# Encoder block on one core: the first pair's difference formed eight steps sooner, its first product a step sooner, a third key buffer and a later carry copy

## The chip, the cores and the metric

The kernel runs on one core of a Trainium2 chip. The metric is the device time of one execution in microseconds (us); the result of a kernel is the median of its runs. Engines are named as the profile names them: PE multiplies matrices (PEld is its loading of weights), DVE, ACT and POOL work on vectors, SP issues transfers.

## The reference

One layer of an encoder. Each row of `z` is normalised and multiplied by one wide matrix; its columns are queries, keys, values and a gate of a windowed attention, and value, gate and output gate of a depthwise convolution of width 31. Both halves are gated, put side by side and multiplied by an output matrix, and `z` is added.

```python
def hybrid_layer(z, norm_w, w_in, q_norm_w, k_norm_w, sink, conv_w, conv_b, ln_w, ln_b, w_out):
    h = rmsnorm(z, norm_w)
    proj = jnp.einsum('bld,de->ble', h, w_in)
    q, k, v, g_att, c_val, c_glu, g_conv = jnp.split(proj, SPLIT_IDX, axis=-1)
    q = rmsnorm(q.reshape(B, L, N_HEADS, HEAD_DIM), q_norm_w)
    k = rmsnorm(k.reshape(B, L, N_KV_HEADS, HEAD_DIM), k_norm_w)
    v = v.reshape(B, L, N_KV_HEADS, HEAD_DIM)
    att = windowed_gqa(q, k, v, sink).reshape(B, L, W_ATT) * jax.nn.silu(g_att)
    cnv = conformer_conv(c_val, c_glu, conv_w, conv_b, ln_w, ln_b) * jax.nn.silu(g_conv)
    mixed = jnp.concatenate([att, cnv], axis=-1)
    return z + jnp.einsum('ble,ed->bld', mixed, w_out)
```

It runs on two inputs, a prompt of 256 rows and a sample of 2048 rows, each with 16 learned rows in front: 18 blocks of 128 real rows. The model width is 1024, there are 8 query heads and 2 key heads of 64, the attention part and the convolution part are 512 wide each. A query sees the learned keys and the keys at most 128 rows away, with a distance penalty by head, and every softmax row has a learned extra logit.

## The kernel before, in words

**Precision.** A product of float32 matrices is made of three matmuls of rounded parts: a factor is split into a high part (a cast, most often by ACT) and a low part (the factor less the high part, by DVE), and high by high, high by low and low by high are summed (`PASSES`). So each operand that PE takes costs a cast on ACT and a subtraction on DVE first.

**Stages.** The rows are taken in two chunks. In each, the projections run on PE: lines 1024 and 1040, 24 matmuls for a block or half block. Beside them DVE makes the convolution, 31 instructions for each of four channel groups (line 1107, one tap each, `y`); they are handed out by credit, some after each projection. The last 113 columns of a group of the first chunk are kept for the second by a copy on ACT into `ycarry` (line 1118).

After a key block's projection, ACT squares and sums (`sqk`), POOL makes the inverse root (`rqk`, lines 179 and 180), DVE forms the normalised keys `kn` (line 1198), PE transposes them (`kt`, line 1208), ACT makes the high part `ks` (line 1210) and DVE the low part (line 1211), and two transfers store them to `kd`. A query block goes the same way up to `qs` (line 1171), which is stored to `qd`.

From 584.9 us (the first `S`) the attention runs, in stages of eight slots: `slot_step` does in each slot the actions of a table (`acts`), one bank of transposes and its products (`bank`, `pv`, line 623, of the block before), the products with the output matrix (`product`, line 729) from the table `JOBS`, and the scores of the block ahead (`scores`). For each head group `kv` of a block: the scores `S` leave PSUM through DVE (line 531, `sb`), ACT makes exponentials (line 543), POOL multiplies by the inverse sums (`pm` line 560, `sb` line 569, four instructions), PE transposes (`pT_c`, `pT_m`, `pT_x`), ACT and DVE split those into `ptiles` (lines 605, 606 and 595 to 597, the last one POOL's), and PE multiplies them with the values (`O`, line 623, with `vc`, `vm` and so on). `merge` then adds the halves (`at`, line 645 on DVE) and multiplies by the gate (line 651 on POOL).

**Output products.** Blocks 2p and 2p+1 are a pair p. Some of the products are made from sums and differences, so that one product serves two blocks: `c1` of one block's convolution part, `s3` of the difference of the two convolution parts, `s2` and `s4` of further differences with the attention parts, `t0`, `t1` and `s1` likewise. `mix_diff` (line 706, POOL) forms the difference into `temp(0)`; `two_parts` (lines 687 and 688) splits an operand on ACT and DVE; the product of `c1` leaves PSUM into `kept(0)` (in the trace `keptFalse`), that of `s2` into `kept(1)`. `merge` of the pair's first block subtracts the difference from its attention part (line 654) and adds the attention part to the convolution part (line 656). The first pair has earlier steps in the table than the others, since no pair is in front of it.

**Order.** A scheduler decides the order of the instructions on the engines from their order in the program and a table of costs, at first on every engine, from the opening of the attention on all but POOL (`MAN1`), later on all but POOL and PE (`MAN2`), which then follow the program. `later(k, f)` puts `f` off by k ticks of the program, `with_rest(f)` holds `f` back until a tile called `rest` exists. `merge` puts itself off by a tick as long as the pair's difference hasn't been issued. Within one engine instructions run in their order, so a waiting one holds all behind it.

Of the kernel before, what the change touches and what calls it, by code (L numbers as in the profile page):

```python
# [12 lines left out]
F32R = mybir.dt.float32r  # L13
BF16 = mybir.dt.bfloat16
AF = mybir.ActivationFunctionType
ALU = mybir.AluOpType
AX = mybir.AxisListType

P = 128
# [111 lines left out]
def hymba_kernel(  # L131
# [61 lines left out]
    def later(k, f):  # L193
        due.setdefault(clock[0] + k, []).append(f)
# [438 lines left out]
    def merge(b, kv):  # L633
        p, r = divmod(b, 2)
        if "rest" not in cst or (kv == 1 and b not in att) or p not in diff:
            return later(1, lambda: merge(b, kv))
        o = opj[b, kv]
        if kv == 0:
            att[b] = pool["b"].tile([P, 4, P], F32, tag="at", name=f"at{b}")
        at = att[b]  # L640
        pr = slice(2 * kv, 2 * kv + 2)
        tmp = pool["b"].tile([64, 4, P], F32, tag="tmp", name=f"tmp{b}_{kv}", bufs=1)
        nc.scalar.copy(tmp, o[64:128])
        for par in range(2):
            nc.vector.tensor_tensor(  # L645
                at[64 * par : 64 * par + 64, pr, :].rearrange("p a (i q) -> p a i q", q=QB),
                o[0:64].rearrange("p i (a c q) -> p c a i q", a=2, c=2)[:, par],
                tmp.rearrange("p i (a c q) -> p c a i q", a=2, c=2)[:, par],
                op=ALU.add,
            )  # L650
        nc.gpsimd.tensor_tensor(at[:, pr, :], at[:, pr, :], gat[b][:, pr, :], op=ALU.mult)  # L651
        part = at[:, pr, :]
        if kv == 0 and r == 0:
            nc.gpsimd.tensor_tensor(temp(1), part, temp(0), op=ALU.subtract)
            total = cnt[b][:, 0:NS, :]
            nc.gpsimd.tensor_tensor(total, total, part, op=ALU.add)
            work = [("t0", part), ("s2", temp(1)), ("s1", total)]
        elif kv == 0:
            nc.gpsimd.tensor_tensor(temp(1), part, temp(1), op=ALU.subtract)
            work = [("t1", part), ("s4", temp(1))]  # L660
        else:
            work = [(("t", r), part)]

        for name, x in work:
            later(2 + (name == "s4"), lambda name=name, x=x: two_parts(name, x))
# [4 lines left out]
    def temp(i):  # L670
        if not temps:
            temps.extend(gp.tile([P, NS, P], F32, tag="sq4", name=f"temp{k}", bufs=2) for k in range(2))
        return temps[i]
# [16 lines left out]
    def with_rest(f):  # L690
        pending.append(f)
        while "rest" in cst and pending:
            pending.pop(0)()
# [8 lines left out]
    def mix_conv(b):  # L702
        nc.gpsimd.tensor_tensor(cnt[b], cnt[b], gct[b], op=ALU.mult)

    def mix_diff(p):
        nc.gpsimd.tensor_tensor(temp(0), cnt[2 * p + 1][:, 0:NS, :], cnt[2 * p][:, 0:NS, :], op=ALU.subtract)
        diff[p] = True

    banks = []
# [51 lines left out]
    for p in range(NB // 2):  # L761
        b0, b1 = 2 * p, 2 * p + 1
        for rel, f in (
            (5 - (p == 0), lambda b1=b1: load_mix(b1)),
            (6 - 2 * (p == 0), lambda b0=b0: load_mix(b0)),
            (9 + 3 * (p == 0), lambda p=p: load_x(p, (0, 1))),
            (11 - 7 * (p == 0), lambda b1=b1: mix_conv(b1)),
            (12 - 8 * (p == 0), lambda b0=b0: mix_conv(b0)),
            (13, lambda p=p: with_rest(lambda: mix_diff(p))),
            (12 + 2 * (p == 0), lambda p=p: load_x(p, (1, 1))),  # L770
            (13 - 4 * (p == 0), lambda b1=b1: two_parts("c1", cnt[b1][:, 0:NS, :])),
            (14, lambda: with_rest(lambda: two_parts("s3", temp(0)))),
            (17, lambda b0=b0: two_parts(("c", 0), cnt[b0][:, NS:4, :])),
            (17, lambda p=p: load_x(p, (0, 0))),
            (20, lambda b1=b1: two_parts(("c", 1), cnt[b1][:, NS:4, :])),
            (18, lambda p=p: load_x(p, (1, 0))),
            (18, lambda p=p: add_kept(p, (1, 1), 0)),
            (20, lambda p=p: add_kept(p, (0, 0), 1)),
            (21, lambda p=p: add_kept(p, (1, 0), 0)),
        ):  # L780
            acts.setdefault(16 * p + rel, []).append(f)
        for rel, name, es in JOBS:
            to = late_jobs if name == "s3" else jobs
            rel -= p == 0 and name == "c1"
            if p == LAST and name in ("t1", (1, 0)):
                for c0 in (0, 256):
                    to.setdefault(16 * p + rel, []).append((p, name, es, c0, 256))
            else:
                to.setdefault(16 * p + rel, []).append((p, name, es))

    def slot_step(s_, slot):
        a, bb = s_, s_ - 1
        has_a, has_b = a < NB, 0 <= bb < NB
        steps = PLAN if has_b else []
        if slot == 0:
            if a + 1 < NB:
                load_q(a + 1)
                load_k(a + 1)
        if slot == 1 and has_b and s_ > 1:
            load_ga(bb)  # L800
        if slot == VSLOT and 0 < a < NB:
            load_v(a)
        t = 8 * s_ + slot
        with_rest(lambda: None)
        for f in acts.get(t, ()):
            f()
        if slot < len(steps) and steps[slot]:
            bank(bb, *steps[slot])
        for job in jobs.get(t, ()):
            product(*job)  # L810
        if has_a:
            scores(a, slot // 4, slot % 4)
        if slot == (3 if s_ == 1 else QSLOT) and a + 1 < NB:
            q_prep(a + 1)
        for job in late_jobs.get(t, ()):
            product(*job)
        tick(2400)
# [44 lines left out]
    if True:  # L862
# [222 lines left out]
        def conv(c, j, part):  # L1085
            yo = 0 if c == 0 else YC
            o0, o1 = (0, YN)
            n = o1 - o0

            def alloc():  # L1090
                yt[c, j] = yp.tile([P, YW], F32, tag="y", name=f"y{c}_{j}")
                if c == 1:
                    nc.scalar.copy(yt[c, j][:, 0:YC], ycarry[:, j, :])

            def tap(k):
                y, u = yt[c, j], us[c, j]
                if k == 0:
                    nc.vector.tensor_scalar(
                        y[:, yo + o0 : yo + o1],
                        u[:, o0:o1],  # L1100
                        cw[:, j, 0:1],
                        cb[:, j : j + 1],
                        op0=ALU.mult,
                        op1=ALU.add,
                    )
                else:
                    nc.vector.scalar_tensor_tensor(  # L1107
                        y[:, yo + o0 : yo + o1],
                        u[:, o0 + k : o1 + k],
                        cw[:, j, k : k + 1],  # L1110
                        y[:, yo + o0 : yo + o1],
                        op0=ALU.mult,
                        op1=ALU.add,
                    )
                if k == TAPS - 1:
                    left[c, part] -= 1
                    if c == 0:
                        nc.scalar.copy(ycarry[:, j, :], y[:, YN - YC : YN])

            conv_q[j % 2].append((0, alloc))  # L1120
            if c == 0:
                nc.gpsimd.tensor_copy(carry[:, j, :], us[0, j][:, UWID - 30 : UWID])
            left.setdefault((c, part), NJ)
            for k in range(TAPS):
                conv_q[j % 2].append((1.04 * n + 135, lambda k=k: tap(k)))
# [58 lines left out]
        def kv_block(ws, g, o, rows, b):  # L1184
# [21 lines left out]
            def fin2():  # L1206
                pt = psum.tile([P, 512], F32, tag="d", name=f"kt{b}")
                nc.tensor.transpose(pt[:, :rows], kn[:rows].rearrange("p a e -> p (a e)"), ident[:rows, :rows])
                ks = sp.tile([P, 2 * P], F32R, tag="ks", name=f"ks{b}")
                nc.scalar.mul(ks[:, :rows], pt[:, :rows], kscale[:, 0:1])  # L1210
                nc.vector.scalar_tensor_tensor(
                    ks[:, rows : 2 * rows], pt[:, :rows], kscale[:, 0:1], ks[:, :rows], op0=ALU.mult, op1=ALU.subtract
                )
                to = (kmd if b < 0 else kd[b]).rearrange("(h p) k l n -> p h k (l n)", h=2)
                for kv in range(KV):
                    part = ks[HD * kv : HD * kv + HD, : 2 * rows].bitcast(F32)
                    store(to[:, :, kv, :], part.unsqueeze(1).to_broadcast([HD, 2, 2 * rows]))
# [264 lines left out]
```

## Time and profile before

| what | us |
|---|---|
| the runs | 945.50, 946.75, 1397.23 |
| their median | 946.75 |
| the profiled execution, as a whole | 944.26 |
| its span, first to last instruction | 942.5 |
| PE busy | 929.3 |
| DVE busy | 782.4 |
| ACT busy | 448.5 |
| POOL busy | 370.0 |

A row of the timeline has the start in us, the length of the row in us, the engine, the line, the operation, the tiles written and read with their shape, how many instructions the row holds, and in brackets the idle time of the engine just ahead of it with what ended that. Instructions of an engine overlap a little, so the spacing from start to start is shorter than the lengths. The granted clock of PE is 1.000 in this execution.

### The profile page before, as it was taken

To read this page: it belongs to the slowest core of one execution; us is meant where nothing else is said; L and a number is where in the kernel's file an instruction comes from. 1 tells how busy PE (TensorE), PEld (TensorE's weight loads), DVE (VectorE), ACT (ScalarE), POOL (GpSimd) and SP (SyncE) were. 2 spreads that over 40 slices of the span, in tenths; PEclk is the share of its full clock that TensorE was granted. 3 is DMA by queue.
4 is the path that set the end of the run, shared out by engine and by line. 5 is a ranking of instruction groups with operands and counts; after the bars stand their busy time and mean duration, and the time that the engine had idled before them with its cause. 6 is when DMAs were issued, how large, how long until landed. Compare 5 with 4: busy or idle time off the path is not lost.

```text
span 942.5 us, 16872 instructions
## 1 busy us (share of the span) xinstructions
PE 929.3 (99%) x5734; PEld 878.1 (93%) x5734; DVE 782.4 (83%) x1340; ACT 448.5 (48%) x1231; POOL 370.0 (39%) x553
## 2 busy tenths in 40 slices
PE   9999999999999999999999999999999999999998
PEld 8999999999899999999999999977888888888887
DVE  5479999998989889999996554689788888897884
ACT  7442221353456770011111355667677676776772
POOL 3320100184668610000000354687665465556644
PEclk9999999999999999999999999999999999999999
DMA  8579775686565562223333688996556665665421
GB/s 297 178 245 361 249 256 179 207 301 229 126 198 172 186 257 90 90 96 111 117 115 115 198 280 271 381 373 186 171 172 190 176 198 152 183 197 169 144 87 55
DMA packets 146342, 182.80 MB, mean 194 GB/s; under 512 B 40944, under 2 KB 106816, under 8 KB 146128
## 3 DMA queue, kind: packets, MB, share of 16 engines
q1 hardware_dynamic: 146256, 181.72, 58.9%
q8 instruction: 45, 0.74, 0.3%
q14 instruction: 41, 0.34, 0.1%
HBM read 115.83 MB, written 65.85 MB: 193 GB/s over the span
## 4 chain that ended last, share of the span: by engine, by line
PE 85%; DVE 5%; DMA 4%; POOL 3%; issue 1%; SPq 1%; ACT 1%; DVEq 0%; POOLq 0%; ACTq 0%
PE pj L1024 41%; PE yb L729 18%; PE pj L1040 10%; PE O L623 5%; PE S L473 4%; DMA cd<-zn 2%; PE pT_m L589 2%; PE pT_c L589 1%; PE pT_x L589 1%; PE warmup L1257 1%; DVE xt L933 1%; DVE y L1107 1%; POOL sb L569 1%; PE qT L473 1%; DMA wraw<-in_w_in 1%
## 5 line engine op out<-in xcount | busy, mean ns | idle before, releaser
L1024 PE MATMUL pj<-xh,ws 128*128 128x384 f32 (+1 forms) x1536 | 396.7, 339 | 0.1
L1107 DVE SCALAR_TENSOR_TENSOR y<-us,cw,y 128x1167 f32<-128x1167 f32 x240 | 329.6, 1425 | 0.5
L1024 PEld LDWEIGHTS pj<-xh,ws 128*128 128x128 f32 x1536 | 280.1, 188 | 0.5 <-ACT xh L1272 0.4
L1024 PE MATMUL pj<-xl,ws 128*128 128x384 f32 (+1 forms) x768 | 260.9, 340 | 0.1
L1040 PE MATMUL pj<-ws,xh 128*128 128x256 f32 (+1 forms) x880 | 164.7, 284 | 4.3 <-DVE qs L1171 2.5
L1024 PEld LDWEIGHTS pj<-xl,ws 128*128 128x128 f32 x768 | 144.1, 188 | 0.5 <-DVE xl L962 0.4
L1040 PEld LDWEIGHTS pj<-ws,xh 128*128 128x128 f32 (+1 forms) x880 | 136.4, 187 | 5.5 <-issue 2.7
L729 PE MATMUL yb<-wo,rest 128*128 128x512 f32 (+1 forms) x498 | 132.1, 399 | 0.0
L1040 PE MATMUL pj<-ws,xl 128*128 128x256 f32 (+1 forms) x440 | 124.2, 282 | 0.0
L729 PEld LDWEIGHTS yb<-wo,rest 128*128 128x128 f32 x498 | 86.9, 189 | 15.3
L1132 ACT ACTIVATE go<-pj 128x384 f32<-128x384 f32 x48 | 23.5, 490 | 151.5 <-PE pj L1024 137.9
L543 ACT ACTIVATE sb<-sb,nm 128x304 f32<-128x304 f32 (+5 forms) x144 | 77.8, 540 | 26.9 <-DVE nm L531 25.1
L179 POOL TENSOR_SCALAR ssk<-ssk 128x2 f32<-128x2 f32 x18 | 10.3, 574 | 204.3 <-ACT sqk L1146 204.1
L569 POOL TENSOR_SCALAR sb<-sb,es 128x304 f32<-128x304 f32 (+5 forms) x144 | 73.0, 524 | 38.4 <-PE pT_x L589 20.6
L1040 PEld LDWEIGHTS pj<-ws,xl 128*128 128x128 f32 (+1 forms) x440 | 82.2, 187 | 0.3
L531 DVE CUSTOM_DVE_ANT_0 sb<-S,bias,vec 128x304 f32<-128x304 f32 (+5 forms) x144 | 73.7, 515 | 9.3 <-PE S L473 8.1
L179 POOL TENSOR_SCALAR ssq<-ssq 128x4 f32<-128x4 f32 (+2 forms) x55 | 30.4, 552 | 92.5 <-ACT xn L887 70.8
L473 PE MATMUL S<-kw,q 128*128 128x304 f32 (+5 forms) x288 | 63.1, 303 | 0.7 <-issue 0.5
L473 PEld LDWEIGHTS S<-kw,q 128*128 128x128 f32 x288 | 52.1, 188 | 11.5 <-ACT keptFalse L747 0.7
L729 PE MATMUL yb<-wo,ptiles 128*128 128x512 f32 x216 | 60.2, 407 | 1.9 <-ACT ptiles L687 1.4
L651 POOL TENSOR_TENSOR at<-at,ga 128x256 f32<-128x256 f32 x36 | 26.6, 740 | 76.0 <-DVE at L645 76.0
L740 DVE TENSOR_TENSOR yo<-yb,yo 128x512 f32<-128x512 f32 (+1 forms) x55 | 37.1, 674 | 15.4 <-PE yb L729 15.2
(162 smaller groups left out, 1456.1 us busy)
## 6 DMA issues: line engine op xcount, KB each, us to landing
wd<-ws SPq DMA_DIRECT2D x36, 512.0 KB, 5.8
ws<-wd SPq DMA_DIRECT2D x36, 512.0 KB, 5.7
wraw<-in_w_in SPq DMA_DIRECT2D x52, 256.0 KB, 6.1
xn<-in_z SPq DMA_DIRECT2D x18, 512.0 KB, 5.4
gd<-go SPq DMA_DIRECT2D x48, 192.0 KB, 2.1
yo<-in_z SPq DMA_DIRECT2D x36, 256.0 KB, 3.4
wo<-wod SPq DMA_DIRECT2D x18, 512.0 KB, 7.8
out_y<-yo SPq DMA_DIRECT2D x35, 256.0 KB, 2.5
```

The lines of the kernel that those rows point to most:

```text
L179: nc.gpsimd.tensor_scalar(src, src, scale, eps, op0=ALU.mult, op1=ALU.add)
L473: r = f(*a, **k)
L531: nc.vector.tensor_tensor_reduce(out=sb[:, n, c0:c1], in0=ps[:, 0:w], in1=cst["bias"][:, kv, at + c0 : at + c1], scale=1.0, scalar=nsnk[:, ...
L543: nc.scalar.activation(sb[:, n, c0:c1], sb[:, n, c0:c1], AF.Exp, bias=nm[:, n : n + 1], scale=-1.0, accum_out=rs[:, n : n + 1],)
L569: nc.gpsimd.tensor_scalar(sb[:, k, a0:a1], sb[:, k, a0:a1], es[:, k : k + 1], 1.0, op0=ALU.mult, op1=ALU.mult)
L589: nc.tensor.transpose(pt[: c1 - c0, n, :], sbt[b, kv][:, n, c0:c1], ident)
L623: nc.tensor.matmul(opj[b, kv][:, n0:n1], t[:r, kv, :], p[:r, n0:n1], start=(k == "c" and i == 0), stop=(k == "x" and i == len(work) - 1),)
L729: nc.tensor.matmul(ps[:, :n], x[mi][:, i, :], w[wi], start=((name, e) in OPENS and k == 0), stop=(done and e == es[-1] and k == 2), skip_g ...
L740: nc.vector.tensor_tensor(y, ps[:, :n], y, op=ALU.add)
L1024: nc.tensor.matmul(ps[:, :n], ws[:, d, wi, P * half_i : P * half_i + P], x[xi][:, d, o : o + n], start=(k == 0), stop=(k == 3 * ND - 1),)
L1040: nc.tensor.matmul(ps[:rows, :UW], x[xi][:, d, o : o + rows], ws[:, d, wi, :], start=(k == 0), stop=(k == 3 * ND - 1),)
L1107: nc.vector.scalar_tensor_tensor(y[:, yo + o0 : yo + o1], u[:, o0 + k : o1 + k], cw[:, j, k : k + 1], y[:, yo + o0 : yo + o1], op0=ALU.mul ...
```

## The change

Five edits.

1. The first pair's difference is issued at step 5 and no longer at step 13, without being held back for `rest`, and it is written into `kept(1)` instead of `temp(0)` (`diff_c`). Line 654 reads it there.
2. The split of the operand of `s3` is issued at step 10 instead of 14 for the first pair, for no pair held back.
3. The first pair's product `c1` is taken two steps sooner than the other pairs', and no longer one.
4. The query preparation of the stage `s_ == 3` is done in slot 5 instead of 6.
5. The copy into `ycarry` is put off by eight ticks and then keeps its program order; the tile `ks` has three buffers and no longer two.

```diff
@@ merge
-            nc.gpsimd.tensor_tensor(temp(1), part, temp(0), op=ALU.subtract)
+            nc.gpsimd.tensor_tensor(temp(1), part, diff_c(p), op=ALU.subtract)
@@
+    def diff_c(p):
+        if p:
+            return temp(0)
+        return kept(1)[:, : NS * P].rearrange("p (j n) -> p j n", n=P)
+
     def mix_diff(p):
-        nc.gpsimd.tensor_tensor(temp(0), cnt[2 * p + 1][:, 0:NS, :], cnt[2 * p][:, 0:NS, :], op=ALU.subtract)
+        nc.gpsimd.tensor_tensor(diff_c(p), cnt[2 * p + 1][:, 0:NS, :], cnt[2 * p][:, 0:NS, :], op=ALU.subtract)
         diff[p] = True
@@ the table of actions
-            (13, lambda p=p: with_rest(lambda: mix_diff(p))),
+            (13 - 8 * (p == 0), lambda p=p: mix_diff(p) if p == 0 else with_rest(lambda: mix_diff(p))),
...
-            (14, lambda: with_rest(lambda: two_parts("s3", temp(0)))),
+            (14 - 4 * (p == 0), lambda p=p: two_parts("s3", diff_c(p))),
@@ the table of products
-            rel -= p == 0 and name == "c1"
+            rel -= 2 * (p == 0 and name == "c1")
@@ slot_step
-        if slot == (3 if s_ == 1 else QSLOT) and a + 1 < NB:
+        if slot == (3 if s_ == 1 else 5 if s_ == 3 else QSLOT) and a + 1 < NB:
@@ conv
-                        nc.scalar.copy(ycarry[:, j, :], y[:, YN - YC : YN])
+                        carry_y = lambda: nc.scalar.copy(ycarry[:, j, :], y[:, YN - YC : YN])
+                        later(8, lambda: tc.keep_in_program_order(carry_y()))
@@ kv_block
-                ks = sp.tile([P, 2 * P], F32R, tag="ks", name=f"ks{b}")
+                ks = sp.tile([P, 2 * P], F32R, tag="ks", name=f"ks{b}", bufs=3)
```

The new lines shift the line numbers of the changed kernel by 5 (from line 706 of before), and by 6 or 7 further down.

How the instructions stand, in three places. First POOL, where the first pair's first `merge` comes. Here `sb_5908` holds the scores of block 1 with its weights `es_0`, `at` is the merged attention part of block 0, `cn_6237` and `cn_6241` are the convolution parts of blocks 1 and 0. Before:

```order
L560 TENSOR_TENSOR pm_0_6684<-sb_5908,es_0_6456 128x128
L569 TENSOR_SCALAR sb_5908<-sb_5908,es_0_6456 128x272
L569 TENSOR_SCALAR sb_5908<-sb_5908,es_0_6456 128x240
L569 TENSOR_SCALAR sb_5908<-sb_5908,es_0_6456 128x208
L569 TENSOR_SCALAR sb_5908<-sb_5908,es_0_6456 128x176
L530 MEMSET sb_5900 128x32
L706 TENSOR_TENSOR temp_6718<-cn_6237,cn_6241 128x256
L651 TENSOR_TENSOR at_6737<-at_6737,ga_6343 128x256
L654 TENSOR_TENSOR temp_6719<-at_6737,temp_6718 128x256
L656 TENSOR_TENSOR cn_6241<-cn_6241,at_6737 128x256
L597 TENSOR_TENSOR ptiles<-ptiles,vec 128x512
```

And in the changed kernel:

```order
L651 TENSOR_TENSOR at_6738<-at_6738,ga_6345 128x256
L560 TENSOR_TENSOR pm_0_6688<-sb_5908,es_0_6458 128x128
L654 TENSOR_TENSOR temp_6745<-at_6738,kept_6299 128x256
L656 TENSOR_TENSOR cn_6241<-cn_6241,at_6738 128x256
L569 TENSOR_SCALAR sb_5908<-sb_5908,es_0_6458 128x272
L569 TENSOR_SCALAR sb_5908<-sb_5908,es_0_6458 128x240
L569 TENSOR_SCALAR sb_5908<-sb_5908,es_0_6458 128x208
L569 TENSOR_SCALAR sb_5908<-sb_5908,es_0_6458 128x176
L530 MEMSET sb_5900 128x32
L597 TENSOR_TENSOR ptiles<-ptiles,vec 128x512
```

The difference is gone from this row; it stands 25 instructions sooner, behind the inverse root `rqq_9`. `merge` no longer waits for it, so its gate (L651), its difference (L654) and its sum (L656) now stand ahead of the four multiplications of `sb_5908`, which were ahead of them.

Second PE at the same place. `yb_6726` before and `yb_6702` now is the bank of the product `c1` (operands `wa`) and of `s3` (operand `wo_6364`, now `wo_6366`); `O_1` is the output of block 0's second head group. Before:

```order
L623 MATMUL O_0_6509<-ptiles,vm 128x512
L589 MATMUL pT_m_6693<-ident,sb_5904 128x128 x4
L623 MATMUL O_1_6701<-ptiles,vc_5912 128x512 x2
L585 MATMUL pT_x_6724<-ident,pm_1_6462 128x128
L729 MATMUL yb_6726<-wa_6297,ptiles 128x512 x3
L729 MATMUL yb_6726<-wa_6341,ptiles 128x512 x3
L473 MATMUL S_1_2_6734<-kw_5892,q_1_6353 128x208 x2
L473 MATMUL S_1_3_6752<-kw_5892,q_1_6353 128x176 x2
L623 MATMUL O_1_6701<-ptiles,vm_5913 128x512 x2
L589 MATMUL pT_c_6767<-ident,sb_5908 128x128 x4
L473 MATMUL S_0_0_6775<-kw_5891,q_2_6621 128x176 x2
L729 MATMUL yb_6726<-wo_6364,ptiles 128x512 x6
```

And in the changed kernel:

```order
L623 MATMUL O_0_6511<-ptiles,vm 128x512
L734 MATMUL yb_6702<-wa_6297,ptiles 128x512 x3
L734 MATMUL yb_6702<-wa_6343,ptiles 128x512 x3
L589 MATMUL pT_m_6697<-ident,sb_5904 128x128 x4
L623 MATMUL O_1_6713<-ptiles,vc_5912 128x512 x2
L585 MATMUL pT_x_6733<-ident,pm_1_6464 128x128
L473 MATMUL S_1_2_6735<-kw_5892,q_1_6355 128x208 x2
L473 MATMUL S_1_3_6753<-kw_5892,q_1_6355 128x176 x2
L623 MATMUL O_1_6713<-ptiles,vm_5913 128x512 x2
L589 MATMUL pT_c_6768<-ident,sb_5908 128x128 x4
L473 MATMUL S_0_0_6776<-kw_5891,q_2_6625 128x176 x2
L734 MATMUL yb_6702<-wo_6366,ptiles 128x512 x6
```

The six matmuls of `c1` went ahead of the transposes `pT_m` and the two products with `vc`; `pT_c` of block 1 (which reads the multiplied `sb_5908`) still stands ahead of `s3`.

Third ACT, 15 us sooner in the program, where `qr_14` is a query block just projected and `pT_c` and `pT_m` belong to block 0. Before:

```order
L552 ACTIVATE es_1_6247<-nm_1_6245,vec 128x4
L1165 COPY qr_14_6502<-pj_6477 128x256
L1141 ACTIVATE sqq_14_6505<-pj_6477 128x256
L605 CAST ptiles<-pT_c_6449 128x512
L605 CAST ptiles<-pT_m_6515 128x512
```

And in the changed kernel:

```order
L552 ACTIVATE es_1_6247<-nm_1_6245,vec 128x4
L687 CAST ptiles<-kept_6299 128x256
L1171 COPY qr_14_6504<-pj_6479 128x256
L1147 ACTIVATE sqq_14_6507<-pj_6479 128x256
L605 CAST ptiles<-pT_c_6451 128x512
L605 CAST ptiles<-pT_m_6517 128x512
```

The cast of the high part of `s3` now stands here, ahead of the query copy and of the two casts that PE's products with `vc` and `vm` need; before it stood behind them all.

## The prediction

> **What bounds the kernel now.** I began with the page: how much of the span is PE busy?
>
> ```profile
> span 942.5 us, 16872 instructions
> PE 929.3 (99%) x5734; PEld 878.1 (93%) x5734; DVE 782.4 (83%) x1340; ACT 448.5 (48%) x1231; POOL 370.0 (39%) x553
> ```
>
> PE is the bound, with 99% of the span. The change takes no matmul away and adds none, so it can only touch PE's idle time, which is 942.5 - 929.3 = 13.2 us in all. A measurement of this kernel tells about 2% from no change, here 18.9 us. Even with every idle moment gone the time would not leave that band, so the question is how many of the 13 us go. The waits of PE, largest first (total, times, longest):
>
> ```profile
> PE pj L1040 <- DVE qs L1171: 2.5, 2, 2.1
> PE pj L1040 <- ACT ycarry L1118: 1.5, 1, 1.5
> PE yb L729 <- ACT ptiles L687: 1.4, 1, 1.4
> ```
>
> These look like the aims of the edits: the carry copy, the operand of `s3`, and a query block that is behind a key block's ring of buffers. For each I looked in the timeline for what really ends last there. The rows shown from here on are picked from the timeline. Where a row of PE begins late, the loss in the stream is a little more than the idle time it shows, because the row before it no longer overlaps; I take idle time plus 0.2 as the loss.
>
> **The carry copy (edit 5, first half).** Around 245 us:
>
> ```profile
> 241.27 4.11 DVE L1107 SCALAR_TENSOR_TENSOR y<-us,cw,y 128x1167 f32<-128x1167 f32 x3
> ...
> 245.30 0.28 DVE L1198 TENSOR_TENSOR kn<-pj,rqk 128x128 f32<-128x128 f32 x1
> 245.41 0.29 ACT L1118 COPY ycarry<-y 128x113 f32<-128x113 f32 x1 [0.30 <-DVE y L1107]
> ...
> 245.72 0.36 PE L1040 MATMUL pj<-ws,xh 128*128 128x256 f32 x1 [1.53 <-ACT ycarry L1118]
> ```
>
> The copy does end last, at 245.70, but PE takes a PSUM bank of a key block here, and what frees it is `kn`, which ends at 245.58 behind three taps of DVE (4.11 us) that run without a gap. Nothing PE needs comes from `ycarry`. Putting the copy off takes 0.29 us from ACT in front of the squares of the next blocks, and those have time; DVE has the same order of taps and `kn` here as before. Value 0; upper end 0.1 (245.70 - 245.58), lower end 0. Its other copy in the table is followed, ten us on, by the longest wait:
>
> ```profile
> 289.37 4.89 POOL L962 TENSOR_TENSOR xl<-xt,xh 128x384 fp32r<-128x384 f32 x4
> ...
> 295.09 1.99 POOL L180 TENSOR_TENSOR rqq<-ssq,half 128x4 f32<-128x4 f32 x2
> ...
> 298.57 0.36 PE L1040 MATMUL pj<-ws,xh 128*128 128x256 f32 x1 [2.11 <-DVE qs L1171]
> ```
>
> That `qs` needs `rqq`, and POOL makes it only after four splits of the next rows' input (4.89 us). Neither is touched, so these 2.1 + 0.2 us stay. Value 0; upper end 0.3, the length of the copy (0.29) that ACT may hold the squares up by.
>
> **The third buffer of `ks` (edit 5, second half).** With two buffers ACT waits until the store of the block two before has landed:
>
> ```profile
> 265.55 1.98 POOL L180 TENSOR_TENSOR rqq<-ssq,half 128x4 f32<-128x4 f32 x2
> ...
> 266.19 0.37 ACT L1210 ACTIVATE ks<-kt,kscale 128x128 fp32r<-128x128 f32 x1 [3.61 <-DMA kd<-ks]
> ...
> 266.59 0.35 DVE L1211 SCALAR_TENSOR_TENSOR ks<-kt,kscale,ks 128x128 fp32r<-128x128 f32 x1 [1.18 <-ACT ks L1210]
> ...
> 266.85 0.41 DVE L1171 TENSOR_TENSOR qs<-pj,rqq 128x256 f32<-128x256 f32 x1
> ...
> 267.42 0.36 PE L1040 MATMUL pj<-ws,xh 128*128 128x256 f32 x1 [0.43 <-DVE qs L1171]
> ```
>
> This is the one place where that wait reaches PE: ACT stood 3.61 us, DVE's low half 1.18 us behind it, `qs` behind that, and PE 0.43 us behind `qs`. The third buffer takes ACT's wait away. Then `qs` waits for the next cause, its `rqq`, the first of the two in the POOL row, done at about 265.55 + 0.99 = 266.54. So `qs` starts at 266.55 instead of 266.85: **0.3 us** gained. Bounds: 0 (POOL's end is rough) and 0.6 (0.43 + 0.2, all of it).
>
> **The difference and `s3` (edits 1 to 3).** Before, PE stands three times at the first pair:
>
> ```profile
> 612.61 0.84 DVE L645 TENSOR_TENSOR at<-O,tmp 64x256 f32<-64x256 f32 x2
> ...
> 612.75 0.51 PE L623 MATMUL O<-ptiles,vc 128*128 128x512 f32 x1 [0.56 <-DVE ptiles L606]
> ...
> 613.50 0.40 POOL L560 TENSOR_TENSOR pm<-sb,es 128x128 f32<-128x128 f32 x1 [3.38 <-DVE at L645]
> ...
> 614.00 1.73 POOL L569 TENSOR_SCALAR sb<-sb,es 128x272 f32<-128x272 f32 x4
> ...
> 615.52 0.60 PE L589 MATMUL pT_c<-ident,sb 128*128 128x128 f32 x4
> ...
> 615.76 0.73 POOL L706 TENSOR_TENSOR temp<-cn,cn 128x256 f32<-128x256 f32 x1
> ...
> 616.45 0.73 POOL L651 TENSOR_TENSOR at<-at,ga 128x256 f32<-128x256 f32 x1
> ...
> 617.32 0.39 ACT L687 CAST ptiles<-temp 128x256 fp32r<-128x256 f32 x1
> ...
> 617.76 0.74 PE L729 MATMUL yb<-wo,ptiles 128*128 128x512 f32 x2 [1.44 <-ACT ptiles L687]
> ...
> 617.93 0.73 POOL L656 TENSOR_TENSOR cn<-cn,at 128x256 f32<-128x256 f32 x1
> ...
> 618.12 0.82 DVE L688 TENSOR_TENSOR ptiles<-temp,ptiles 128x256 fp32r<-128x256 f32 x1
> ...
> 618.63 1.22 POOL L597 TENSOR_TENSOR ptiles<-ptiles,vec 128x512 fp32r<-128x512 f32 x1
> ...
> 619.00 1.20 PE L729 MATMUL yb<-wo,ptiles 128*128 128x512 f32 x4 [0.51 <-DVE ptiles L688]
> ...
> 620.04 0.39 PE L623 MATMUL O<-ptiles,vm 128*128 128x512 f32 x1
> ```
>
> The losses are 0.56 at `O` (low half of `pT_c` late), 1.44 at `s3`'s first matmuls (its high half) and 0.51 at the others (its low half); with 0.2 each, about 3.1 us. All three causes go: `c1` now stands ahead of the late `O` (six matmuls at a spacing of 0.74 - 0.51 = 0.23, 1.4 us in all, more than 0.76), and `s3`'s parts are ready ten us early. So far the change would gain 3.1 us.
>
> But look at the POOL rows. From 613.50, just behind DVE's `at` (ends 613.45), POOL runs without a gap to 618.63 + 1.22 = 619.85, and the last of it, L597, is what `O` with `vm` at 620.04 needs: the stream of PE is tied to POOL's queue at that end. The change takes one thing out of it, the difference (spacing 615.76 to 616.45, 0.69), and moves the merge's three instructions ahead of the four multiplications of `sb`. So by the same durations: gate 613.5 to 614.2, `pm` to 614.7, L654 (like L651 and L656) to 615.4, L656 to 616.1, four multiplications to 617.85, memset, L597 to 619.1. And `pT_c` of block 1 needs those multiplications. It ran at 615.52 before; PE will be there at 615.52 - 0.76 = 614.8 and finish it at about 617.9, so it stands about 2.2 us less what the first three transposes fill. Behind it in PE's queue are one score and the six matmuls of `s3`: 617.9 + 0.3 + 6 x 0.23 = 619.6. Then `O` with `vm` starts at 619.6 where it was 620.04.
>
> So the wait at `s3` turns into a wait at `pT_c`, and the gain is **0.5 us**. Bounds: 3.1, if the multiplications are no later than before; and below nothing -1.0, next paragraph.
>
> **What the early difference adds.** ACT's cast of it stands right ahead of what PE needs for block 0:
>
> ```profile
> 598.94 1.02 POOL L180 TENSOR_TENSOR rqq<-ssq,half 128x4 f32<-128x4 f32 x1
> 598.99 0.37 ACT L1165 COPY qr<-pj 128x256 f32<-128x256 f32 x1 [0.83 <-PE pj L1040]
> ...
> 599.53 0.59 ACT L605 CAST ptiles<-pT_c 128x512 fp32r<-128x512 f32 x1
> ...
> 602.44 0.39 PE L623 MATMUL O<-ptiles,vc 128*128 128x512 f32 x1
> ```
>
> POOL comes to the difference behind this `rqq` and a memset, at about 600.1, and needs 0.7: done at 600.8. ACT, which was free, now waits for it; its cast takes a spacing of 0.4, the copy and the square 0.54 (598.99 to 599.53), and the cast of `pT_c` ends at 600.8 + 0.4 + 0.54 + 0.59 = 602.3, 2.2 us later than before. `O` with `vc` at 602.44 needs it; it now stands two projection matmuls further down, some 0.2 us. The cover is 0.14 + 0.2, about 0.35 us. I take 0; if it is gone, each further us is PE's. A second inverse root in front of the difference (1.3 us, from the row of 1.02 with its 0.19 and gaps) would cost 1.0.
>
> One sign that POOL's and DVE's rows lengthen each other is in the rows already shown: the low half at 618.12 took 0.82 beside POOL's sum, an equal one later, with no sum of POOL beside it, took half:
>
> ```profile
> 620.05 0.41 DVE L688 TENSOR_TENSOR rest<-temp,rest 128x256 fp32r<-128x256 f32 x1
> ```
>
> [...]
>
> **The query preparation (edit 4).**
>
> ```profile
> 654.24 0.51 PE L473 MATMUL S<-kw,q 128*128 128x304 f32 x2 [0.54 <-issue]
> ...
> 655.31 1.23 POOL L597 TENSOR_TENSOR ptiles<-ptiles,vec 128x512 fp32r<-128x512 f32 x1
> ...
> 656.59 0.51 PE L623 MATMUL O<-ptiles,vm 128*128 128x512 f32 x1 [0.44 <-POOL ptiles L597]
> ```
>
> The wait at 654.24 is for the split of block 4's queries and goes with an earlier slot, 0.54 + 0.2. But two us on PE waits for POOL's L597, at the end of a run of POOL that has hardly a gap (span, busy time and instructions of POOL in that stretch):
>
> ```profile
> 641.85:656.54 14.69, 14.34 (x21) 1.00 0.62 182
> ```
>
> Nothing of that run is moved, so PE comes there 0.7 sooner and waits 0.7 longer. Value 0, ends 0 and 0.8.
>
> **The sum.** 0 + 0.3 + 0.5 + 0 + 0 = 0.8 us gained. The profiled execution took 944.26 us (1.8 more than its span) and would take 943.5. The two runs near it are 945.5 and 946.75, so the three executions lie 2.5 us apart and their middle is 945.5: 945.5 - 0.8 = **944.7 us**.
>
> **Rivals.**
>
> *A, the waits really vanish* (15%). If the multiplications of `sb` aren't on the path (DVE's `at` earlier, or POOL's spans shorter than they look) the three waits at the first pair are worth 3.1, the third buffer 0.6, the queries 0.7: 4.4 us, and 941.1. For it: POOL's idle 3.38 us ahead of 613.50, which the gate could use if DVE's `at` came sooner. Against it: `at` has its own row at 612.61, behind `O` and two DVE rows that aren't moved. With the waits at 245.72 and 298.57 gone as well (1.7 and 2.3) it would be 8.4 us, 937.1; DVE's taps and POOL's splits speak against that.
>
> *B, slower* (20%). ACT's wait for the early difference, in front of the casts of `pT_c` and `pT_m`. It decides as soon as the difference lands 0.35 us later than I have it. If one more inverse root goes first, PE loses 1.0, and if a DVE row is stretched as the low half above was (0.82 against 0.41) 0.4 more; less the gain at the other places, 0.8, that is 0.6 us slower, 946.1; with the `pT_c` wait a full us worse than reckoned, 947.1. For it: behind the waiting cast stand the query copy, which frees a projection bank, and the casts, and PE's `O` waits for these. Against it: ACT stood 0.83 us ahead of the copy at 598.99 anyway.
>
> *C, no gain at all* (10%). The spans of POOL are what they are, `qs` waits for an `rqq` that ends later than its row's middle, and the first pair's chain loses its 0.5 to one more memset. 945.5.
>
> The forecast as worked out, within half a us of 944.7, has 55%.
>
> **Range and chances.** The bounds of the terms: best 0.1 + 0.3 + 0.6 + 3.1 + 0.8 = 4.9 gained (940.6), worst 0.5 - 1.0 - 1.0 = 1.5 lost without the gains elsewhere (947.0). The middle of three runs moves by up to 1.25 either way without any change (945.5 to 946.75). I give 940.5 to 947.5; A's far end of 937 stays out. Slower or faster by over 2% (926.6 or 964.4 from 945.5, or the same from the median 946.75) isn't reached by any case: 97% within 2%, 2% faster, 1% slower, for what the trace doesn't show.
>
> **What would show it.** In the changed kernel's profile PE busy should stay at 929 and its idle time go from 13.2 to about 12.4. Right, step by step: no wait of PE on ACT's `ptiles` of line 687 and none at `O` near 612; in its place a wait of about 2 us of PE at `pT_c` (L589) released by POOL's `sb` (L569); the `qs` wait at 267 shorter by 0.3; the wait at 245.7 still there, now put down to `kn`; the one at 298.6 still 2.1; the one at 654 gone and that at 656.6 up to 1.1. Wrong, if PE has no wait at `pT_c` near 616 (then A), or if a wait appears at 602 to 604 at `O`, released by ACT or DVE `ptiles` (then B).

## The result: 948.2 us, slower by half a per cent

| | before | changed |
|---|---|---|
| median, us | 944.03 (19 runs) | 948.22 (19 runs) |
| ratio, 95% interval | | 1.0046, 1.0038 to 1.0055 |
| profiled execution: span, us | 942.5 | 945.4 |
| its mean granted clock | 1.000 | 0.996 |

The 4.2 us are well inside the 2% band and well outside the uncertainty of these runs. Forecast was a gain of 0.8 us, with a range up to 947.5. One execution of the changed kernel (1850 us) and two of before (1397 and 1132 us) were far off; they stand in these medians and are left out of the ratio.

The page of the changed kernel differs from that of before in a row that the prediction doesn't use, the granted clock of PE in 40 slices:

```profile
span 945.4 us, 16870 instructions
PE 930.4 (98%) x5734; PEld 877.3 (93%) x5734; DVE 782.4 (83%) x1340; ACT 448.0 (47%) x1231; POOL 373.6 (40%) x553
PEclk9999999999999999999999999989999999999999
```

One slice has an 8, and PE, with the same matmuls, is busy 1.1 us longer. PE's waits (total, times, longest):

```profile
PE pj L1045 <- DVE qs L1177: 1.9, 1, 1.9
PE pT_c L589 <- POOL sb L569: 1.6, 1, 1.6
PE pj L1045 <- ACT ycarry L1123: 1.5, 1, 1.5
PE lnu L273 <- DVE zn L267: 1.5, 2, 1.0
...
PE pj L1045 <- ACT sqq L1152: 0.4, 1, 0.4
PE yb L734 <- DVE rest L688: 0.4, 1, 0.4
PE S L473 <- issue: 0.4, 1, 0.4
```

The waits of `s3` on ACT and DVE are gone and the wait at `pT_c` is there, as forecast. Three are new that I had not forecast: `lnu` for `zn`, `yb` for a low half of line 688, and `pj` for ACT's `sqq` at the place of the third buffer. And here is the first pair, PE and then POOL:

```profile
614.77 0.50 PE L623 MATMUL O<-ptiles,vm 128*128 128x512 f32 x1 [0.34 <-DVE ptiles L606]
616.88 1.88 PE L589 MATMUL pT_c<-ident,sb 128*128 128x128 f32 x4 [1.61 <-POOL sb L569]
618.41 0.71 PE L473 MATMUL S<-kw,q 128*128 128x176 f32 x2
618.92 2.83 PE L734 MATMUL yb<-wo,ptiles 128*128 128x512 f32 x6
621.54 0.63 PE L623 MATMUL O<-ptiles,vm 128*128 128x512 f32 x1
```

```profile
613.47 0.73 POOL L651 TENSOR_TENSOR at<-at,ga 128x256 f32<-128x256 f32 x1 [3.78 <-PE pT_x L585]
614.16 0.40 POOL L560 TENSOR_TENSOR pm<-sb,es 128x128 f32<-128x128 f32 x1
614.52 0.73 POOL L654 TENSOR_TENSOR temp<-at,kept 128x256 f32<-128x256 f32 x1
615.21 0.73 POOL L656 TENSOR_TENSOR cn<-cn,at 128x256 f32<-128x256 f32 x1
615.91 2.32 POOL L569 TENSOR_SCALAR sb<-sb,es 128x272 f32<-128x272 f32 x4
```

POOL's queue runs as worked out (gate at 613.47, multiplications from 615.91, where 613.5 and 616.1 had been put), but its four multiplications take 2.32 us instead of 1.73. And the six matmuls of `s3` take 2.83 us where six of `c1` took 1.65 before. The granted clock of the two stretches, after span, busy time and instructions of PE, says why:

```profile
613.01:616.42 3.41, 1.82 (x9) 1.00 1.03 412
616.42:623.25 6.83, 6.27 (x18) 0.50 1.04 410
```

After a stretch in which PE waits twice, the clock is halved for 6.83 us. Half of what PE did from 618.4 (when `pT_c` was through) to 623.25 is lost: 4.8 / 2 = 2.4 us.

To see where the rest goes, the same transposes are compared in the two traces (start in the changed kernel less start in before, us):

```
start in before      234   293   303   526   578   604   623   640   660   927
offset             -1.11 -1.13 -1.32 -0.45 +0.11 -0.14 +2.33 +2.26 +2.78 +2.88
```

The first 1.1 us are in the load at the start, which no edit touches. Lost are 0.9 between 303 and 526, 0.6 between 526 and 578, 2.5 between 604 and 623 and 0.5 between 640 and 660; gained 0.2 at 298 and 0.25 before 604. One execution of each is a small base, so the experiments were timed in five rounds, with the kernel before on the same chip.

### The profile page after: what moved, and what is told of

Its sections match the earlier page's. It is cut to its first block, busy times and chain, and to the rows that moved or that the text cites. A ratio compares the mean times of both kernels' runs of the same rounds, so it can differ in the third digit from the quotient of the medians.

```text
span 945.4 us, 16870 instructions
## 1 busy us (share of the span) xinstructions
PE 930.4 (98%) x5734; PEld 877.3 (93%) x5734; DVE 782.4 (83%) x1340; ACT 448.0 (47%) x1231; POOL 373.6 (40%) x553
## 5 line engine op out<-in xcount | busy, mean ns | idle before, releaser
L179 POOL TENSOR_SCALAR ssq<-ssq 128x4 f32<-128x4 f32 (+2 forms) x55 | 34.1, 620 | 93.0 <-ACT xn L892 71.0
L651 POOL TENSOR_TENSOR at<-at,ga 128x256 f32<-128x256 f32 x36 | 26.5, 737 | 79.4 <-DVE at L645 75.7
```

Of the source, the lines that this page charges most:

```text
L179: nc.gpsimd.tensor_scalar(src, src, scale, eps, op0=ALU.mult, op1=ALU.add)
```

## The experiments

**Two halves of the change.** Edits 1 to 3 alone, which are the first four pieces of the diff above (`diff_c`, the two rows of the table, `c1`'s step):

```diff
-            (13, lambda p=p: with_rest(lambda: mix_diff(p))),
+            (13 - 8 * (p == 0), lambda p=p: mix_diff(p) if p == 0 else with_rest(lambda: mix_diff(p))),
...
-            rel -= p == 0 and name == "c1"
+            rel -= 2 * (p == 0 and name == "c1")
```

> Edits 1 to 3 alone (early difference, early operand of s3, c1 a step sooner). Clock theory: in the changed kernel PE's waits at the first pair are joined into one stretch of about 3 us with little work (1.6 us idle at pT_c), after which the granted clock is 0.5 for 6.8 us, which costs half of that, 3.4 us; the waits themselves get about 1 us shorter. So this kernel should be 2.3 to 2.8 us slower than before, with a mean clock of 0.996 to 0.998 and a slice at half clock near 617 us. Rival (the half clock is an accident of the profiled execution, the waits decide): 0.5 us faster than before, clock 1.000.

Measured: 945.84, ratio 1.0019 (1.0008 to 1.0030), 1.8 us slower; the granted clock was 0.998 or less in 12 executions of 12. The clock theory has the sign and the clock right and the size somewhat high; the rival is out.

Edits 4 and 5 alone:

```diff
-        if slot == (3 if s_ == 1 else QSLOT) and a + 1 < NB:
+        if slot == (3 if s_ == 1 else 5 if s_ == 3 else QSLOT) and a + 1 < NB:
...
+                        later(8, lambda: tc.keep_in_program_order(carry_y()))
...
+                ks = sp.tile([P, 2 * P], F32R, tag="ks", name=f"ks{b}", bufs=3)
```

> Edits 4 and 5 alone (query slot, carry copy, third key buffer). Order theory: the extra time outside the first pair comes from these: PE's lnu transposes and the stages around them are put in another order between 293 and 345 us, where a new wait of 1.0 us for zn stands, another of 0.45 at 570 us, and 0.5 at 660 us, less 0.2 at 267 and 297: 1.5 to 1.9 us slower than before, clock 1.000. Rival (these are chance of one execution, only the named waits move): 0.3 us faster than before.

Measured: 945.61, ratio 1.0025 (1.0011 to 1.0039), slower by 1.5 us by the medians and 2.4 by the ratio. The order theory has the sign; its size is reached only with some help of the clock (executions at 1.000 are 1.2 us above before's at 1.000). One piece of it is not from these edits: the wait for `zn` near 570 us is in 12 of the 14 traces, with 2.33 us in that of edits 1 to 3 alone, and only before and the kernel without edit 3 lack it. The clock was not full in all executions, against what was expected; in the profiled one it fell twice (windows of 20 us: span, busy, instructions, clock):

```profile
280.00:300.00 20.00, 17.59 (x142) 0.95 0.53 167
300.00:320.00 20.00, 20.00 (x143) 0.97 0.45 145
620.00:640.00 20.00, 18.89 (x89) 0.91 0.92 332
```

Both are places of before's program, the wait for `qs` at 298 and that for `s3`'s operand at 620. So before has this fall too, in some of its executions. The granted clock of the single executions, all kernels together:

| kernel | executions | 1.000 | 0.999 | 0.998 or less |
|---|---|---|---|---|
| before, beside the experiments | 102 | 47 | 16 | 39 |
| changed | 18 | 0 | 0 | 18 |
| edits 1 to 3 | 12 | 0 | 0 | 12 |
| edits 4 and 5 | 12 | 6 | 1 | 5 |
| third buffer | 10 | 1 | 1 | 8 |
| later copy | 11 | 6 | 1 | 4 |
| query slot | 11 | 6 | 2 | 3 |
| changed, wait filled with 28 passes | 11 | 11 | 0 | 0 |
| changed, wait filled with 8 passes | 12 | 5 | 1 | 6 |
| changed, gate held back | 12 | 7 | 1 | 4 |
| changed without edit 3 | 12 | 9 | 1 | 2 |
| edits 1 and 2 | 12 | 11 | 1 | 0 |
| edits 1 and 2, gate held back | 12 | 11 | 1 | 0 |
| edits 1 to 3, gate held back | 11 | 9 | 1 | 1 |

In before, an execution at 0.998 takes 0.9 to 1.5 us more than one at 1.000 (medians 944.80 and 943.69, 944.28 and 943.35, 945.00 and 943.55 in the three sets). The mean gives an estimate of how long the clock was halved: the 6.83 us at half of the changed kernel's trace take 0.5 x 6.83 / 945 = 0.0036 off it, half of them, 3.41 us, 0.0018. Of the changed kernel's 18 executions 8 are at 0.998, 8 at 0.996 and two lower. Where the clock fell is on record for the profiled executions alone.

**Is it the clock?** The wait is left as it is and PE is given work in it, matmuls into the bank that the transposes then overwrite:

```diff
+        if (b, k, kv) == (1, "c", 0):
+            for _ in range(14):
+                nc.tensor.matmul(pt[:, 0, :], ident, ident, start=True, stop=True)
```

> The changed kernel with 14 additional small matmuls into the bank of pT_c just ahead of its transposes, where PE waits for POOL's multiplications; they are overwritten by the transposes and leave the result as it is. Clock theory: PE is kept busy in the wait, the clock stays at 1.000, and 3.4 us come back: 944.8 where the changed kernel has 948.2. Rival (the wait itself costs the time): no change from the changed kernel, or slower by the 0.2 us by which the extra matmuls may outlast the wait.

Measured: 946.28, ratio 1.0023 (1.0014 to 1.0031) against 1.0046 (1.0038 to 1.0055) without the filling: 1.9 us back by the medians (2.2 by the ratios) for extra work, and full clock in 11 of 11. PE's order is the changed kernel's but for the 28 added passes. The rival is out. The size was put too high: the first 2.0 us of the half clock fall into PE's wait for POOL, where it costs nothing, and 8 of the 18 executions were at 0.998, half of the loss that was reckoned with. The place with the filling:

```profile
615.82 3.29 PE L587 MATMUL pT_c<-ident 128*128 128x128 f32 x28
618.94 0.60 PE L593 MATMUL pT_c<-ident,sb 128*128 128x128 f32 x4
619.30 0.44 PE L474 MATMUL S<-kw,q 128*128 128x176 f32 x2
619.57 1.58 PE L738 MATMUL yb<-wo,ptiles 128*128 128x512 f32 x6
```

The wait for POOL is as long as without (from 615.8 to 618.9), yet `s3` takes 1.58 us and not 2.83. A smaller filling:

```diff
-            for _ in range(14):
+            for _ in range(4):
```

> The changed kernel with 4 extra matmuls in front of pT_c (8 passes of 0.117 us, 0.94 us) in place of 14 (28 passes, 3.3 us). Theory that the clock goes by the idle share in some microseconds: part of the wait filled is enough in part of the executions, mean clock between 0.997 and 1.000, median 946.3 to 947.5. Rival (any wait for POOL at this place halves it): 948.2, every execution below 0.999.

Measured: 946.64, ratio 1.0032 (1.0018 to 1.0046); full clock in 5 of 12, 0.998 or less in 6. The rival, every execution below 0.999, is out. That the filled part decides isn't shown by this run: in its profiled execution (0.996) the clock is full at the first pair and fell at 299.24 and 575.72, behind waits of 2.34 us for `qs` and 1.98 us for `zn`. Where it fell in the others isn't known.

**Is it the order on POOL?** The gate is pinned behind what precedes it in the program, the four multiplications among it:

```diff
-        nc.gpsimd.tensor_tensor(at[:, pr, :], at[:, pr, :], gat[b][:, pr, :], op=ALU.mult)
+        gate = nc.gpsimd.tensor_tensor(at[:, pr, :], at[:, pr, :], gat[b][:, pr, :], op=ALU.mult)
+        if (b, kv) == (0, 0):
+            tc.keep_in_program_order(gate)
```

> The changed kernel with the gate of the first merge kept behind the four multiplications of block 1 on POOL, as before; the difference stays early. Theory: pT_c no longer waits, the wait of PE moves to O with vm, which needs POOL's L597 at the end of the same queue: about 2.2 us in one piece. If the clock stays at 1.000 the first pair is 0.5 to 0.9 us shorter than before and the kernel comes to 945.2 (3.0 below the changed one); if one piece of 2.2 us also halves the clock, it stays at 947.5 to 948.5. Rival (the order on POOL doesn't matter): 948.2.

Measured: 945.42, ratio 1.0016 (1.0005 to 1.0027), 2.8 us below the changed kernel by the ratios. The multiplications are back at their old length and the wait sits where it was expected:

```profile
616.13 1.74 POOL L569 TENSOR_SCALAR sb<-sb,es 128x272 f32<-128x272 f32 x4
...
620.09 1.22 POOL L597 TENSOR_TENSOR ptiles<-ptiles,vec 128x512 fp32r<-128x512 f32 x1
```

```profile
618.29 1.59 PE L736 MATMUL yb<-wo,ptiles 128*128 128x512 f32 x6
621.37 0.51 PE L623 MATMUL O<-ptiles,vm 128*128 128x512 f32 x1 [1.49 <-POOL ptiles L597]
```

One piece of 1.49 us, and no half clock here (this execution had its fall at 298). From 604 to 623 it took 0.25 us less than before, not 0.5 to 0.9 less.

Undoing only `c1`'s step in the changed kernel:

```diff
-            rel -= 2 * (p == 0 and name == "c1")
+            rel -= p == 0 and name == "c1"
```

> The changed kernel without the step of c1 (edit 3 undone): its six matmuls stay between pT_x and the scores. They are then in the stretch in which PE waits. Clock theory: there is less idle time in any 3.4 us, so the half clock comes in fewer executions than in the changed kernel, where all had it: median 946.0 to 947.0, mean clock above 0.998. POOL's order at the place differs too (the gate behind pm, the other two behind the multiplications). Rival (c1 plays no part): 948.2, half clock in all.

Measured: 945.10, ratio 1.0021 (1.0012 to 1.0030), full clock in 9 of 12. That is more of a recovery than expected (946.0 to 947.0). The kernel is as slow as edits 4 and 5 alone; so edits 1 and 2 cost nothing, and `c1`'s step costs the rest where it stands with them. It does so in two ways at once: six matmuls leave the stretch, and POOL's order changes. Without it only the gate goes ahead of the multiplications, with it L654 and L656 too.

**Edits 4 and 5 one by one.** The third buffer, the later copy, the query slot, each alone (the diffs are single lines of the pair above):

```diff
+                ks = sp.tile([P, 2 * P], F32R, tag="ks", name=f"ks{b}", bufs=3)
```

> Third key buffer alone. It moves PE's transposes lnu and lnt between 293 and 345 us exactly as edits 4 and 5 together do. Order theory: 0.5 to 0.8 us slower than before (edits 4 and 5 together were 1.5 slower in all executions, 1.2 in those at full clock; half of a us of it is the query slot). Rival (the buffer is free, it removes a wait): 0 to 0.3 us faster.

```diff
+                        later(8, lambda: tc.keep_in_program_order(carry_y()))
```

> Later carry copy alone. The same order of PE as with the third key buffer alone, another one of ACT. Order theory: 0.5 to 0.8 us slower than before, like that one. Rival (each is free by itself): 0.

```diff
+        if slot == (3 if s_ == 1 else 5 if s_ == 3 else QSLOT) and a + 1 < NB:
```

> Query slot alone. The offset between the traces grows by 0.5 us between 640 and 660 us in each kernel with this edit and not in the one without: a new wait of 0.4 us at 660 us for a low half (line 688) that DVE does later. Theory: 0.5 us slower than before. Rival (the forecast): 0.

Measured: 945.59, 1.0027 (1.0015 to 1.0039); 945.82, 1.0024 (1.0012 to 1.0035); 944.29, 1.0009 (1.0000 to 1.0017). The order theory has the sign in all three; for the first two the size is above its 0.5 to 0.8 us, in part by the clock (third buffer: 8 of 10 executions at 0.998). In both traces it fell behind the wait for `s3`'s operand (at 621.83 and 619.73), which before has too. The interval of the third reaches down to no change; for it the offset below speaks. The first two move PE's order in the same way, so both together don't cost more than one. What it costs is a wait that all eight kernels with either of them have near 340 us (0.48 to 1.39), and none of the others; in the first two:

```profile
341.49 0.63 PE L273 MATMUL lnu<-ident,zn 128*128 128x128 f32 x4 [1.39 <-DVE zn L267]
```

```profile
339.89 0.63 PE L273 MATMUL lnu<-ident,zn 128*128 128x128 f32 x4 [1.36 <-DVE zn L267]
```

In the changed kernel one sees what `zn` stands behind on DVE, a weight split that waits for ACT:

```profile
338.29 0.69 DVE L397 TENSOR_TENSOR wos<-wor,wos 128x512 fp32r<-128x512 f32 x1 [1.98 <-ACT wos L396]
338.90 0.81 DVE L267 TENSOR_SCALAR zn<-lnt,mv 128x512 f32<-128x512 f32 x1
```

The offset to before grows from 303 to 526 us by 0.5 to 1.9 us in the eight kernels (mean 1.0), and by -0.06 to 0.01 in the five without. The query slot brings this wait, which before does not have:

```profile
658.47 0.73 PE L729 MATMUL yb<-wo,rest 128*128 128x512 f32 x2 [0.41 <-DVE rest L688]
```

The offset grows there by 0.5 in every kernel with edit 4 and by nothing in those without.

**The change without its costs.** Edits 1 and 2 alone, then with the gate held back, then edits 1 to 3 with the gate held back:

```diff
-            (14, lambda: with_rest(lambda: two_parts("s3", temp(0)))),
+            (14 - 4 * (p == 0), lambda p=p: two_parts("s3", diff_c(p))),
```

> Edits 1 and 2 alone: c1 where it was, no edit 4 or 5. On POOL only the gate stands ahead of the four multiplications. With the changed kernel less edit 3 the stretch from 607 to 623 us took 0.2 us less than before and the clock was full in 9 executions of 12. Theory: this is the change without its costs, 0.1 to 0.5 us faster than before, mean clock above that of before. Rival (the early difference costs by itself, through ACT's wait): 0.5 us or more slower.

```diff
+            tc.keep_in_program_order(gate)
```

> Edits 1 and 2 with the gate kept behind the multiplications: POOL's order is that of before without the difference. PE then waits for L597 at the end of POOL's queue, which is 0.7 us shorter. Theory: as with edits 1 and 2 alone, 0 to 0.7 us faster than before. Rival: the wait in one piece halves the clock in more executions, 0.5 to 1.5 us slower.

```diff
+            tc.keep_in_program_order(gate)
...
+            rel -= 2 * (p == 0 and name == "c1")
```

> Edits 1 to 3 with the gate kept behind the multiplications, no edit 4 or 5. With edits 4 and 5 this was 1.4 us slower than before, of which they cost 1.5. Theory: 943.6 to 944.1, the same as before within 0.3 us, and full clock in more than half of the executions, where edits 1 to 3 without it had none and were 1.8 us slower. Rival (c1's step costs the time, not the order on POOL): 1.0 to 1.8 us slower than before.

Measured beside a before of 944.02: 943.05, ratio 0.9988 (0.9978 to 0.9998); 942.61, 0.9983 (0.9973 to 0.9993); 942.71, 0.9983 (0.9973 to 0.9992). All three beat both kernels, before by 1.0 to 1.4 us, which is more than expected. `c1`'s step costs nothing once the gate is held back, so the last rival is out. By the medians a third to a half of the gain is the clock: 14 of before's 35 executions in this set were at 0.998, one of the 35 of these three kernels; before's at 1.000 have a median of 943.55, 0.5 below that of all. In the best one PE's longest wait at the place is

```profile
618.64 0.50 PE L623 MATMUL O<-ptiles,vm 128*128 128x512 f32 x1 [1.30 <-POOL ptiles L597]
```

## Why the prediction was wrong

**The base.** I took 945.5 from three executions; before's median over 19 runs is 944.03. On that base the forecast would have been 943.2. So the terms are 5.0 us off, and the base hid 1.5 of them.

**"So the wait at `s3` turns into a wait at `pT_c`, and the gain is 0.5 us."** The first half held to 0.2 us, by POOL's rows. The second half failed on two things. POOL's multiplications took 2.32 and not 1.73 us, which alone eats the 0.5. And the step took a wait of PE to cost its length. It did not look at the clock, which had been 1.000 throughout in the one execution there was. The changed kernel's waits, 0.34 and 1.61 us with one matmul between them, stand where the clock falls in its trace (616.42), and none of its 18 executions had the full clock; filling the wait gave back 1.9 us with the wait unchanged. That before loses the clock too, in 39 of 102 executions, could not be seen in its one profile; the clocks of its other executions show it.

The traces show how long the clock stays halved: 6.83 us in the changed kernel's, and about half of that, 3.4 us, from 622.2 in that of edits 4 and 5 and from 298.4 in that of the changed kernel with the gate held back. In the changed kernel's the granted clock changes at 616.42, 623.25 and 944.10, 2 and 94 times 3.413 us apart; with the 8 passes the two falls, at 299.24 and 575.72, are 81 times 3.413 us apart. In the 3.41 us ahead of the fall PE was busy for 1.82; ahead of that at 622 with edits 4 and 5 for 1.46, ahead of the two with the 8 passes for 1.07 and 1.43.

The busy time of such a stretch does not tell by itself. The changed kernel's trace has one with 1.74 (295.57 to 298.98) and kept its clock behind it. Before's, whose clock falls only behind its last instruction, at 942.74, has this one at the first pair and kept its clock:

```profile
615.06:618.48 3.42, 1.98 (x12) 1.00 1.04 413
```

The same waits have 1.46 in a stretch from 615.60 to 619.01 of that execution. The stretches with 1.82, 1.74 and 1.98 lie a multiple of 3.413 us from a change of the clock in their trace, that with 1.46 does not. Whether that position matters, and why some executions of one kernel lose the clock and others keep it, no run shows. What the clock follows stays open.

**"The third buffer of `ks`: 0.3 us."** No gain is seen: PE waits 0.45 us at this place, now for ACT's `sqq`, where it had waited 0.43 for `qs`; the offset moves by 0.02.

**"The carry copy: value 0."** As a wait it was 0: the wait is still 1.5 and still put down to `ycarry`, and the 298 wait is still 1.9. But both edits moved something that the prediction did not cost: the scheduler put PE's `lnu` and `lnt` transposes between 293 and 345 us in another place. That piece of the order was not shown and not priced. It cost about 1 us (edits 4 and 5 together, 1.5).

**"The query preparation: value 0, ends 0 and 0.8."** Both ends were on the wrong side. The wait at 654 shrank from 0.54 to 0.40 only, so something other than the query split ended last there (the trace names nothing, "issue"); and DVE, with the split moved, brought a low half late for `yb` at 660. 0.5 to 0.7 us lost.

**Rival B, slower through ACT's wait for the early difference.** Slower came out, by another way. ACT did wait 2.58 us, but the difference was there sooner than reckoned:

```profile
599.94 0.41 ACT L687 CAST ptiles<-kept 128x256 fp32r<-128x256 f32 x1 [2.58 <-POOL kept L711]
...
600.79 0.59 ACT L605 CAST ptiles<-pT_c 128x512 fp32r<-128x512 f32 x1
```

```profile
602.17 0.39 PE L623 MATMUL O<-ptiles,vc 128*128 128x512 f32 x1
```

PE's `O` begins with no wait. The cover held, and edits 1 and 2 alone are 1.0 us faster than before by the medians (0.4 among executions at full clock).

**The sum after the fact**, by differences of medians: edits 4 and 5 1.5; the clock 1.9; both together 3.4 of 4.2. The 0.8 left are of the size of the longer multiplications and the waits of `c1`'s order on POOL; no run separates them further. The split is rough: by the ratios the two terms are 2.4 and 2.2 and leave nothing of 4.3, and the first has falls of the clock of its own in it (1.2 at full clock). Edits 1 to 3 alone (1.8) and 4 and 5 alone (1.5) add up to 3.3 as well.

One sentence of the description ahead of the prediction is also wrong: POOL's order is not that of the program alone. Moving `c1`'s step, a matter of PE, changed the order of the gate, L654 and L656 against the multiplications, and an instruction to keep the program order moved the gate.

## What to carry to other kernels

Waits that stand close together can cost more than their length (here 0.34 and 1.61 us, with 6.83 us at half the clock, of which I put the loss at 2.4): look at the stretch of some microseconds around them, and at the clock of many executions, not only at the length of the wait in one profile. Where a scheduler sets the order, an edit that takes away an idle wait still costs whatever it reshuffles; list every place where the order of the bound engine changes and price each, before those that the edit was made for. When the chain of one engine sets the end (POOL here), hold back what isn't needed first: pinning one gate behind four multiplications gave back 2.8 of the 4.2 us.

## What the runs showed of the hardware

The clock of PE fell to half for 6.83 us at waits of 0.34 and 1.61 us in the changed kernel's trace, and in none of its 18 executions was it full throughout; before's is at 0.998 in 39 of 102. The mean granted clock is 0.998 or 0.996 in seven of the 14 profiled executions. In the changed kernel's the fall came behind 3.41 us with 1.82 us of PE busy; before's kept its clock behind stretches of that length with 1.98 and with 1.46. With 28 passes in the wait (3.29 us) it was full in 11 of 11 executions; with 8 passes in 5 of 12, and the profiled one of the others lost it elsewhere.

POOL's multiplications, 1.73 us for four, took 2.32 while DVE ran these beside them:

```profile
616.14 0.41 DVE L688 TENSOR_TENSOR rest<-temp,rest 128x256 fp32r<-128x256 f32 x1
616.47 0.36 DVE L555 TENSOR_TENSOR es<-es,rs 128x4 f32<-128x4 f32 x1
...
616.96 0.57 DVE L688 TENSOR_TENSOR rest<-cn,rest 128x256 fp32r<-128x256 f32 x1
```

In before and with the gate held back none of line 688 ran beside them, and they took 1.73 and 1.74; with one such row beside them they took 1.89 (edit 3 undone) and 2.01 (edits 1 and 2). In the prediction's rows it was DVE's that took longer, 0.82 beside POOL's sum against 0.41. No run took DVE's rows away alone, so what lengthened POOL's is not shown.
